# A fourth raw buffer, a third pair and a clock with measured durations in a recorded transformer kernel

## The chip, the cores and the metric

The kernel runs on one core of a Trainium2 chip. One launch computes the whole network. Times are device microseconds (us). The kernel before took 2119.27 us, the median of 3 runs (2117.88 to 2119.61); the profile was taken on one more execution of it, which took 2115.18 us.

The engines are called by their names and by the short names of the profile: TensorE (PE for its matmuls, PEld for its weight loads), VectorE (DVE), ScalarE (ACT), GpSimd (POOL) and SyncE (SP), which issues the DMA transfers.

## The reference

256 latent tokens and 256 context tokens, 1024 channels, float32, two layers. Each layer has a mixer and a PEER stage (a table of 16384 one-row experts per layer), and both are modulated by a vector that comes from the conditioning:

```python
for i in range(DEPTH):                                 # DEPTH = 2
    mod = (c_act @ ada_w[i] + ada_b[i])                # six vectors of 1024: shift, scale, gate, twice
    h = rmsnorm(x, norm1_w[i]) * (1.0 + sc1) + sh1
    if i % 2 == 0:
        y, y_c = mixer_ab(h, h_c, ...)                 # gated DeltaNet (both directions) and attention
    else:
        y = fourier_mix(h) @ w_out_f[j]
    x = x + g1 * y
    x = x + g2 * peer(rmsnorm(x, norm2_w[i]) * (1.0 + sc2) + sh2, peer_wq[i], ...)
return rmsnorm(x, final_norm_w)

def peer(h, w_q, sub_keys, u_tab, v_tab):              # for each block of 128 tokens
    q = (hb @ w_q).reshape(128, 8, 2, 128)
    s = einsum('thpd,hpnd->thpn', q, sub_keys)         # 8 heads, 2 halves, 128 keys each
    s1, i1 = top_k(s[:, :, 0], 16)
    s2, i2 = top_k(s[:, :, 1], 16)
    top_s, pos = top_k(all 256 sums s1 + s2, 16)       # 16 experts for each head
    gate = softmax(top_s)
    act = gelu(einsum('td,thkd->thk', hb, u_tab[idx]))
    return einsum('thk,thkd->td', gate * act, v_tab[idx])
```

## The kernel before

**Stages.** The mixer of layer 0 fills the first 465 us or so. It multiplies with `w_in` (29 weight tiles), builds the modulation vectors from `ada_w` (tiles that pass through the buffers `mraw`), inverts the triangular matrices of the DeltaNet chunks on VectorE, computes the attention, merges, scans, and multiplies with `w_out`. Then come the PEER stage of layer 0 (up to about 1255 us), the Fourier mixer of layer 1, and the PEER stage of layer 1 up to the end. The two PEER stages are the same code and the same order of instructions.

**A weight tile.** All large matrices come in tiles of 128 x 1024 float32, in one `Stream` (line 200) in the order of their use. SyncE's DMA brings a tile into a raw buffer (`loads`, line 214). ScalarE copies it, rounded, to the first half of a pair; VectorE subtracts that from the raw tile and so gets the second half (`cuts`, line 225). This subtraction is called a cut here. `mm3` (line 275) then issues 24 matmuls for the tile: high weights by high and by low activations, and low weights by high activations. A raw buffer comes free after its cut, a pair's halves after their last matmuls. There are three raw buffers and two pairs; a PEER stage lends the stream one more pair, called `wide` in the rows, until it has its own use for it.

**A PEER stage** (line 1396) takes 16 tiles of `w_q` and 128 of the table u, then 128 of the table v. While TensorE runs through the tiles of u, VectorE makes the selection, one generator for each block of 128 tokens (`select`, line 1522). For each head it does two top-16 searches over 128 scores and one over 112 candidates, each with `max`, `max_index` and `match_replace`. It then turns positions into key numbers and normalises the gates. At its end three transposes on TensorE bring the two key numbers and the gates into the buffer `pT`; they are called T0 for token block 0 and T1 for block 1. After that `weigh` (line 1616) makes one-hot factors of `pT` on VectorE, four operations of 128 x 1024 float16 for 8 tokens, TensorE multiplies them, and `spread` (line 1644) multiplies the result into DD, which holds the activations of the experts by expert columns. Columns of u that are stored later are multiplied by their weight when they are stored (`activations`, line 1509). So the fewer columns are stored when `weigh` runs, the smaller are the products of `spread` and the more multiplications `activations` makes.

**What sets the order.** Each engine works through its instructions in the order in which the program recorded them. The program is written as generators ("chains"); `Lanes.run` (line 65) always resumes the chain whose clock stands lowest. The clocks come from `took` (line 98), which gives every recorded instruction an estimated duration. An estimate that is too long or too short therefore changes no arithmetic, only the order on the queues. Two factors stretch VectorE's estimates, `PACE` (line 31): 1.35 in `select`, 1.1 in `weigh`. Every instruction is issued from one line of a helper (133 in this kernel, 127 in the changed one), so lines don't tell instructions apart in the profile; buffers and shapes do.

Of the kernel before, what the change touches and what calls it, by code (L numbers as in the profile page):

```python
# [11 lines left out]
F16 = mybir.dt.float16  # L12
# [13 lines left out]
AHEAD = 6  # L26
SUMMED = 6
LN_EXP = "natural_log_exp_and_others"


PACE = 1.35, 1.1


EARLY = dict(cc=(KC, 2), ada_b=(2, 48), norm1=(2, KC), norm2=(2, KC), norm_f=(KC,))
LATER = dict(conv=(12, 3), unit=(3,), unitw=(2,), headw=(2,), lam=(4,), ones64=(128,), tri=(128,), rot=(128,),
# [14 lines left out]
class Lanes:  # L50
# [5 lines left out]
    def __init__(self, nc):  # L56
        self.nc, self.free, self.cur, self.waiting = nc, {}, None, []
        self.tensor, self.vector, self.scalar, self.gpsimd, self.sync = (
            Lane(self, n) for n in ("tensor", "vector", "scalar", "gpsimd", "sync"))
# [38 lines left out]
    def took(self, eng, op, args):  # L98
        now = self.cur.after(eng) if self.cur else 0.0
        n = max([math.prod(a.shape[1:]) for a in args[:2] if hasattr(a, "shape")], default=0)  # L100
        if eng == "sync":
            self.free[eng] = max(self.free.get(eng, 0.0), now) + n * args[0].shape[0] * 4 / 360e3
            return
        if eng == "tensor":
            n = math.prod(args[0].shape[1:])
            if op == "transpose":
                d = 0.11
            elif args[2].dtype == F32:
                d = n / 2400 if args[0].shape[0] == 32 else n / 600 if n >= 128 else 0.42
            else:  # L110
                d = n / 2400
        elif eng == "vector":
            d = n / (1920 if all(a.dtype == F16 for a in args[:3] if hasattr(a, "dtype")) else 960)
            d = max(d + (0.115 if op.startswith("ma") else 0.07), 0.12)
        else:
            d = n / (1200 if eng == "scalar" else 600) + 0.1
        if self.cur and eng == "vector":
            d *= self.cur.pace
        self.free[eng] = max(self.free.get(eng, 0.0), now) + d
        if self.cur:  # L120
            self.cur.t, self.cur.eng = self.free[eng], eng
# [16 lines left out]
class Chain:  # L138
    def __init__(self, gen, t, low, ground):
        self.gen, self.t, self.low, self.ground, self.on, self.eng = gen, t, low, ground, [], None  # L140
        self.pace = 1.0

    def wait(self, t, eng):
        if t > self.t:
# [55 lines left out]
class Stream:  # L200


    def __init__(self, c, pool, sources):
        self.c, self.n, self.sources = c, 0, sources
        lanes = c.nc
        self.raws = lanes.stock([c.t(pool, [128, 1024], tag=f"raw{i}") for i in range(3)])
        self.parts = [lanes.stock(x) for x in zip(*(c.pair_tiles(pool, f"pair{i}") for i in range(2)))]
        self.raw, self.tile = {}, {}
        self.loaded, self.cut = lanes.events(2, len(sources))
        self.begin = lanes.events(2)  # L210
        lanes.add(self.loads(), ground=True)
        lanes.add(self.cuts(), ground=True)
# [1183 lines left out]
def peer(c, layer, xT, shift, g2, coming, A):  # L1396

    nc = lanes = c.nc
    banks, stream = c.banks, c.stream
    with c.tc.tile_pool(name=f"peer{layer}", bufs=1) as dp:  # L1400
# [7 lines left out]
        x = c.scaled  # L1408
# [3 lines left out]
        def region(j, n):  # L1412
            return DD[:, j:j + n, :].rearrange("p a b -> p (a b)")
# [107 lines left out]

        def select(tb):

            lanes.cur.pace, lanes.cur.low = PACE[0], "vector"
            w = Scratch(region(80 + 12 * tb, 12))
            rep, cand, rep2 = w(128), w(112), w(112)
            tv = w(256).rearrange("p (h s a) -> p h s a", h=8, s=2)
# [62 lines left out]
            n = 2048  # L1590
            while n >= 512:
# [5 lines left out]
                                    op=OP.add)  # L1597
# [18 lines left out]
        def weigh(i):  # L1616


            yield pk
            lanes.cur.pace = PACE[1]  # L1620
            oa, bh, ob = late["onehots"][i]
            for g in range(i, NT // 8, 2):
                i1, i2, hi, lo = (pT[:, n, g * 8:g * 8 + 8].rearrange("p (g t) -> p g t", g=4).unsqueeze(2)
                                  .broadcast_to([128, 4, 128, 2]) for n in range(4))
                iota = c.iota.unsqueeze(1).broadcast_to([128, 4, 128, 2])
                nc.vector.tensor_tensor(oa, i1, iota, op=OP.is_equal)
                yield
                nc.vector.tensor_tensor(ob, i2, iota, op=OP.is_equal)
                yield
                nc.vector.tensor_tensor(bh, ob, hi, op=OP.mult)  # L1630
                yield
                nc.vector.tensor_tensor(ob, ob, lo, op=OP.mult)
                yield
                for f in range(2):
                    ps = yield from banks.take()
                    pt = ps.rearrange("p (t j) -> p t j", t=4)
                    for t in range(4):
                        a, b, d = (x[:, 2 * f + t // 2, :, t % 2] for x in (oa, bh, ob))
                        nc.tensor.matmul(pt[:, t], a, b, start=True, stop=False)
                        nc.tensor.matmul(pt[:, t], a, d, start=False, stop=True)  # L1640
                    lanes.add(spread(2 * g + f, pt, ps))
                    yield

        def spread(e, pt, ps):
            yield ek[e - 1] if e else None
            there = sorted(stored)
            n = 2 * len(there)
            assert there == list(range(len(there)))
            ts = slice(e * 4, e * 4 + 4)
            pt = pt.rearrange("p t j -> p j t")  # L1650
            if n < 128:
                nc.scalar.activation(DD[:, n:, ts], pt[:, n:], AF.Copy, scale=1.0 / GSC)
            nc.vector.scalar_tensor_tensor(DD[:, :n, ts], pt[:, :n], 1.0 / GSC, DD[:, :n, ts], op0=OP.mult, op1=OP.mult)
            banks.give(ps)
            weighed[0] += 4
            ek[e].set()
# [75 lines left out]
        for gen in (normalised(), load_keys(), queries(), weights(), select(0), select(1), weigh(0), weigh(1),  # L1732
                    *(scores(hd) for hd in range(8))):
            lanes.add(gen)
# [154 lines left out]
```

## Time and profile before

| | kernel before |
|---|---|
| median of 3 runs | 2119.27 us (2117.88 to 2119.61) |
| profiled execution, its own time | 2115.18 us |
| span of that execution | 2113.4 us |
| TensorE busy | 2063.5 us, 98% |
| VectorE busy | 1549.2 us, 73% |
| ScalarE busy | 1022.1 us, 48% |
| read from memory | 366.71 MB, 174 GB/s over the span |

The profile describes one execution. The span runs from its first to its last instruction, and the execution's own time is a little longer. Engines work side by side, so busy times don't add up. TensorE is busy in all but 2% of the span, and most of what VectorE and ScalarE do lies beside its matmuls. A window of the trace gives the busy time of each engine in a stretch, the number of instructions that started there, and the clock that TensorE was granted, as a share of its full speed. A timeline gives the instructions of an engine in order, each with its start and duration, and in brackets how long the engine had been idle before it and which engine ended that.

### The profile page before, as it was taken

How to read it: one execution, taken by the hardware profiler on the slowest of the kernel's cores; microseconds unless marked ns; L12 is line 12 of the kernel's file. 1: busy time of each engine (PE TensorE's matmuls, PEld its weight loads, DVE VectorE, ACT ScalarE, POOL GpSimd, SP SyncE). 2: the span in 40 equal slices, each digit the busy share in tenths (PEclk: the TensorE clock that was granted, in tenths of full speed). 3: DMA queues.
4: the chain of work that ended last, by engine and by line, in shares of the span. 5: the costliest groups of instructions: out<-in, count | busy, mean ns of one | idle time of the engine just before them, and what ended most of it. 6: DMA issues, size and time to landing. Idle time of an engine off the chain costs nothing.

```text
span 2113.4 us, 43065 instructions
## 1 busy us (share of the span) xinstructions
PE 2063.5 (98%) x17732; PEld 1933.9 (92%) x17732; DVE 1549.2 (73%) x3039; ACT 1022.1 (48%) x1542; POOL 82.8 (4%) x122
## 2 busy tenths in 40 slices
PE   7999989999999999999999999999999999999998
PEld 3566658989999999999999989999999999999997
DVE  3479978879998999565555556999899956555554
ACT  4443344155545444554444545554544455444453
POOL 3000023000000000000000000000000000000000
PEclk8999999999999999999999999999999999999999
DMA  7655671045565444665655543556544466666553
GB/s 300 213 180 169 232 240 38 1 133 180 189 198 170 142 149 151 198 212 196 192 195 194 193 160 116 172 190 199 170 141 149 150 199 211 195 194 193 196 192 118
DMA packets 102549, 370.65 MB, mean 175 GB/s; under 512 B 11696, under 2 KB 12976, under 8 KB 101968
## 3 DMA queue, kind: packets, MB, share of 16 engines
q1 hardware_dynamic: 102352, 367.90, 53.0%
q8 instruction: 138, 2.26, 0.4%
q14 instruction: 59, 0.48, 0.1%
HBM read 366.71 MB, written 1.15 MB: 174 GB/s over the span
## 4 chain that ended last, share of the span: by engine, by line
PE 79%; DVE 10%; DMA 6%; ACT 3%; issue 1%; POOL 0%; SPq 0%; POOLq 0%; ACTq 0%; DVEq 0%
PE bank L133 79%; DMA raw<-in_u_dram 3%; DVE wide_lo L133 3%; DVE pair L133 2%; DVE wide L133 2%; DMA mraw<-in_ada_w_dram 2%; DVE DD L133 1%; DVE area L133 1%; ACT pair L133 1%; DMA area<-in_ctx_dram 1%; ACT wide L133 0%; ACT DD L133 0%; DMA area<-in_ada_w_dram 0%; ACT bank L133 0%; DVE a L133 0%
## 5 line engine op out<-in xcount | busy, mean ns | idle before, releaser
L133 ACT ACTIVATE pair<-raw 128x1024 fp32r<-128x1024 f32 x376 | 399.1, 1062 | 435.2 <-PE bank L133 342.9
L133 DVE TENSOR_TENSOR pair<-raw,pair 128x1024 fp32r<-128x1024 f32 x376 | 458.1, 1219 | 182.8 <-ACT pair L133 167.1
L133 PE MATMUL bank<-h,pair 128*128 128x256 f32 x4464 | 557.4, 280 | 0.0
L133 PEld LDWEIGHTS bank<-h,pair 128*128 128x128 f32 x4464 | 528.8, 188 | 0.2 <-DVE pair L133 0.2
L133 PE MATMUL bank<-wide,pair 128*128 128x256 f32 (+1 forms) x3456 | 417.1, 277 | 0.0
L133 PEld LDWEIGHTS bank<-wide,pair 128*128 128x128 f32 x3456 | 405.4, 188 | 0.6
L133 PE MATMUL bank<-wide,h 128*128 128x256 f32 x2880 | 336.6, 276 | 0.0
L133 PEld LDWEIGHTS bank<-wide,h 128*128 128x128 f32 x2880 | 331.3, 188 | 0.0
L133 PE MATMUL bank<-h,wide 128*128 128x256 f32 x2160 | 264.5, 277 | 0.0
L133 PEld LDWEIGHTS bank<-h,wide 128*128 128x128 f32 x2160 | 253.7, 188 | 0.0
L133 DVE TENSOR_TENSOR h<-raw,h 128x1024 fp32r<-128x1024 f32 x120 | 147.0, 1225 | 140.1 <-ACT h L133 140.1
L133 ACT ACTIVATE h<-raw 128x1024 fp32r<-128x1024 f32 x120 | 127.4, 1062 | 161.8 <-PE bank L133 149.2
L133 PE MATMUL bank<-S,pair 128*128 128x256 f32 (+1 forms) x888 | 195.5, 362 | 4.2 <-POOL S L133 2.5
L133 PEld LDWEIGHTS bank<-S,pair 128*128 128x128 f32 x888 | 138.8, 199 | 52.3 <-issue 29.9
L133 ACT ACTIVATE DD<-bank 128x512 f32<-128x512 f32 (+25 forms) x284 | 107.6, 394 | 95.8 <-PE bank L133 92.8
L133 ACT ACTIVATE wide<-raw 128x1024 fp32r<-128x1024 f32 x90 | 95.6, 1062 | 106.7 <-PE bank L133 53.3
L133 DVE TENSOR_TENSOR wide<-raw,wide 128x1024 fp32r<-128x1024 f32 x90 | 109.3, 1214 | 2.3 <-ACT wide L133 2.0
L133 DVE TENSOR_TENSOR wide<-DD,wide 128x512 fp32r<-128x512 f32 x128 | 87.3, 684 | 8.3 <-ACT wide L133 8.2
L133 DVE TENSOR_TENSOR DD<-bank,DD 128x512 f32<-128x512 f32 (+13 forms) x84 | 42.3, 504 | 64.8 <-ACT bank L133 61.2
L133 DVE TENSOR_TENSOR wide_lo<-wide_lo,pT 128x1024 f16<-128x1024 f16 x128 | 85.9, 681 | 0.0
L133 ACT ACTIVATE wide<-DD 128x512 fp32r<-128x512 f32 x128 | 78.6, 615 | 9.5 <-PE bank L133 9.5
L133 POOL TENSOR_TENSOR wide_lo<-wide_lo 128x256 f32<-128x256 f32 x10 | 8.3, 834 | 1591.5 <-ACT wide_lo L133 1590.9
(242 smaller groups left out, 1893.7 us busy)
## 6 DMA issues: line engine op xcount, KB each, us to landing
raw<-in_u_dram SPq DMA_DIRECT2D x256, 512.0 KB, 3.5
raw<-in_v_dram SPq DMA_DIRECT2D x256, 512.0 KB, 4.3
mraw<-in_ada_w_dram SPq DMA_DIRECT2D x84, 512.0 KB, 4.2
raw<-in_wq_dram SPq DMA_DIRECT2D x32, 512.0 KB, 3.5
raw<-in_w_in_dram SPq DMA_DIRECT2D x29, 512.0 KB, 4.3
area<-in_ada_w_dram SPq DMA_DIRECT2D x12, 512.0 KB, 6.3
raw<-in_w_out_ab_dram SPq DMA_DIRECT2D x8, 512.0 KB, 4.5
raw<-in_w_out_f_dram SPq DMA_DIRECT2D x8, 512.0 KB, 3.5
```

Source lines behind the costliest of these rows:

```text
L133: return f(*args, **kw)
```

## The change

Three things change.

The stream gets a fourth raw buffer and a third pair. In a PEER stage four pairs serve the stream while it has `wide`, instead of three.

The memory comes from `dynamic_dma_scratch_size=1024`, an argument of the program's constructor that shrinks the area kept for dynamic DMAs. The kernel has none of these.

In `took` the float32r matmuls count n/2257 us instead of n/2400 for n output columns, `max` gets an overhead of 0.175 us, `max_index` 0.14 and `match_replace` 0.25 in place of 0.115, 0.115 and 0.115, and the two factors of `PACE` go.

```diff
-PACE = 1.35, 1.1
...
             elif args[2].dtype == F32:
                 d = n / 2400 if args[0].shape[0] == 32 else n / 600 if n >= 128 else 0.42
             else:
-                d = n / 2400
+                d = n / 2400 if args[2].dtype == F16 else n / 2257
         elif eng == "vector":
             d = n / (1920 if all(a.dtype == F16 for a in args[:3] if hasattr(a, "dtype")) else 960)
-            d = max(d + (0.115 if op.startswith("ma") else 0.07), 0.12)
+            d = max(d + dict(max=0.175, max_index=0.14, match_replace=0.25).get(op, 0.07), 0.12)
         else:
             d = n / (1200 if eng == "scalar" else 600) + 0.1
-        if self.cur and eng == "vector":
-            d *= self.cur.pace
...
-        self.raws = lanes.stock([c.t(pool, [128, 1024], tag=f"raw{i}") for i in range(3)])
-        self.parts = [lanes.stock(x) for x in zip(*(c.pair_tiles(pool, f"pair{i}") for i in range(2)))]
+        self.raws = lanes.stock([c.t(pool, [128, 1024], tag=f"raw{i}") for i in range(4)])
+        self.parts = [lanes.stock(x) for x in zip(*(c.pair_tiles(pool, f"pair{i}") for i in range(3)))]
...
-            lanes.cur.pace, lanes.cur.low = PACE[0], "vector"
+            lanes.cur.low = "vector"
...
-            lanes.cur.pace = PACE[1]
...
-    nc = bacc.Bacc("TRN2", target_bir_lowering=False, num_devices=1)
+    nc = bacc.Bacc("TRN2", target_bir_lowering=False, num_devices=1, dynamic_dma_scratch_size=1024)
```

The clock and the buffers move instructions on every engine. Three places show how. In the rows, names carry a running number; `h` are the activations, `ident` marks a transpose, and x16 counts equal instructions in a row.

The first is TensorE's queue in the PEER stage of layer 0 around T0, the transposes of `DD` by `ident`. Before:

```order
L133 MATMUL bank_3_66<-h_3819,pair_12_75 128x256 x16
L133 MATMUL bank_3_66<-h_3819,pair_13_76 128x256 x8
L133 MATMUL bank_3_66<-h_3819,wide_4041 128x256 x24
L133 MATMUL bank_5_68<-h_3819,pair_14_77 128x256 x4
L133 MATMUL bank_6_69<-ident_82,DD_3818 128x128 x3
L133 MATMUL bank_5_68<-h_3819,pair_14_77 128x256 x12
```

And in the changed kernel:

```order
L127 MATMUL bank_6_69<-h_3825,pair_13_76 128x256 x16
L127 MATMUL bank_6_69<-h_3825,pair_14_77 128x256 x8
L127 MATMUL bank_6_69<-h_3825,wide_4051 128x256 x24
L127 MATMUL bank_4_67<-ident_85,DD_3824 128x128 x2
L127 MATMUL bank_5_68<-h_3825,pair_15_78 128x256
L127 MATMUL bank_4_67<-ident_85,DD_3824 128x128
L127 MATMUL bank_5_68<-h_3825,pair_15_78 128x256 x15
```

The rows look alike, but from the first score matmul to T0 the queue holds 748 weight-tile matmuls before and 608 now; from T0 to T1 it holds 776 and 649.

The second is VectorE's queue in the selection of that layer, where the cuts (`TENSOR_TENSOR` with a raw buffer) stand between the operations of the top-16 searches. Before:

```order
L133 TENSOR_TENSOR pair_15_78<-raw_10_73,pair_14_77 128x1024
L133 MAX_INDEX DD_3818<-DD_3818 128x8
L133 MAX DD_3818<-DD_3818 128x8
L133 MAX_INDEX DD_3818<-DD_3818 128x8
L133 MATCH_REPLACE DD_3818<-DD_3818 128x128
L133 MAX DD_3818<-DD_3818 128x8
L133 TENSOR_TENSOR pair_13_76<-raw_11_74,pair_12_75 128x1024
```

And in the changed kernel:

```order
L127 TENSOR_TENSOR wide_4051<-raw_11_74,wide_4051 128x1024
L127 MAX_INDEX DD_3824<-DD_3824 128x8
L127 MAX DD_3824<-DD_3824 128x8
L127 MAX_INDEX DD_3824<-DD_3824 128x8
L127 MATCH_REPLACE DD_3824<-DD_3824 128x128
L127 MAX DD_3824<-DD_3824 128x8
L127 MAX_INDEX DD_3824<-DD_3824 128x8
L127 MAX DD_3824<-DD_3824 128x8
L127 MAX_INDEX DD_3824<-DD_3824 128x8
L127 TENSOR_TENSOR pair_16_79<-raw_12_75,pair_15_78 128x1024
```

More operations of the search now stand between two cuts: up to T0 there are 30 cuts before and 26 now, from T0 to T1 32 and 26.

The third is TensorE's queue near the end of the mixer, where the inverse (`area`, 64x64) is transposed. Before, modulation tiles (`mraw`) stand between the transposes:

```order
L133 MATMUL bank_3_66<-ident_82,area_29_108 64x64 x8
L133 MATMUL bank_2_65<-ident_82,area_29_108 64x64 x8
L133 MATMUL bank_7_70<-ident_82,area_29_108 64x64 x8
L133 MATMUL bank_6_69<-mraw_37_116,cact_88 32x256 x4
L133 MATMUL bank_5_68<-ident_82,area_29_108 64x64 x8
L133 MATMUL bank_4_67<-ident_82,area_29_108 64x64 x8
L133 MATMUL bank_6_69<-mraw_36_115,cact_88 32x256 x4
```

In the changed kernel the last modulation tile stands ahead of them, among the products of the attention:

```order
L127 MATMUL bank_6_69<-mraw_40_119,cact_91 32x256 x4
L127 MATMUL bank_7_70<-ident_85,wide_lo_116 128x128 x4
L127 MATMUL bank_4_67<-area_31_110,bq_123 128x512
L127 MATMUL bank_2_65<-ident_85,mrow_117 128x128 x4
L127 MATMUL bank_1_64<-wide_lo_116,area_31_110 128x128 x4
L127 MATMUL bank_6_69<-area_31_110,bq_123 128x512
L127 MATMUL bank_5_68<-ident_85,area_32_111 64x64 x8
L127 MATMUL bank_4_67<-ident_85,area_32_111 64x64 x3
L127 MATMUL bank_7_70<-ident_85,wide_lo_116 128x128 x4
L127 MATMUL bank_4_67<-ident_85,area_32_111 64x64 x5
```

Of the 84 modulation tiles that use the two `mraw` buffers, 45 are used before the last projection matmul of 512 columns in the kernel before and 56 now; behind the last projection matmul stand 10 before and 2 now.

## Rows read from the trace of the kernel before

**Rows 1.** The page's first part: busy us, share of the span, instructions.

```profile
PE 2063.5 (98%) x17732; PEld 1933.9 (92%) x17732; DVE 1549.2 (73%) x3039; ACT 1022.1 (48%) x1542; POOL 82.8 (4%) x122
```

**Rows 2.** A window: its us, busy us (and starts) by engine, clock, DMA share, GB/s.

```profile
850.00:900.00 50.00, 50.00 (x443) 50.00 (x442) 27.80 (x30) 25.38 (x29) 0.00 (x0) 1.00 0.61 193
```

**Rows 3.** Windows of the mixer in which TensorE is idle at times.

```profile
200.00:250.00 50.00, 45.88 (x337) 31.92 (x329) 47.84 (x70) 17.96 (x34) 0.79 (x1) 0.93 0.66 219
250.00:300.00 50.00, 46.05 (x329) 29.27 (x322) 37.17 (x76) 23.36 (x52) 11.76 (x14) 0.93 0.73 249
300.00:350.00 50.00, 45.86 (x446) 35.59 (x445) 43.57 (x94) 25.68 (x58) 18.89 (x32) 1.00 0.37 120
```

**Rows 4.** Windows: selection of block 0, of block 1, one-hot products.

```profile
481.36:568.36 87.00, 87.00 (x760) 86.91 (x759) 82.31 (x280) 47.68 (x64) 0.00 (x0) 1.00 0.57 187
568.36:655.95 87.59, 87.59 (x774) 87.59 (x773) 82.31 (x272) 44.56 (x52) 0.00 (x0) 1.00 0.59 193
...
662.51:837.89 175.38, 173.15 (x1694) 169.12 (x1693) 164.17 (x260) 86.21 (x159) 0.00 (x0) 1.00 0.45 145
```

**Rows 5.** TensorE's timeline: start us, us, instruction (scores, T0, T1, first product).

```profile
478.28 1.95 PE L133 MATMUL bank<-DD 128*128 128x128 f32 x16
...
571.50 0.49 PE L133 MATMUL bank<-ident,DD 128*128 128x128 f32 x3
...
659.99 0.49 PE L133 MATMUL bank<-ident,DD 128*128 128x128 f32 x3
...
670.31 0.63 PE L133 MATMUL bank<-wide_lo 128*128 128x128 f16 x8
```

**Rows 6.** VectorE's timeline: normalisations, copy to pT, a cut, one-hot factors.

```profile
568.07 0.29 DVE L133 TENSOR_TENSOR DD<-DD 128x128 f32<-128x128 f32 x1
...
655.66 0.29 DVE L133 TENSOR_TENSOR DD<-DD 128x128 f32<-128x128 f32 x1
...
660.52 0.43 DVE L133 CAST pT<-bank 128x256 f16<-128x256 f32 x1 [3.00 <-PE bank L133]
...
661.38 1.21 DVE L133 TENSOR_TENSOR pair<-raw,pair 128x1024 fp32r<-128x1024 f32 x1
662.51 0.68 DVE L133 TENSOR_TENSOR wide_lo<-pT,iota 128x1024 f16<-128x1024 f16 x1
...
663.72 0.68 DVE L133 TENSOR_TENSOR wide_lo<-pT,iota 128x1024 f16<-128x1024 f16 x1
```

**Rows 7.** Layer 1, timelines of VectorE and TensorE: normalisation and T0.

```profile
1414.01 0.29 DVE L133 TENSOR_TENSOR DD<-DD 128x128 f32<-128x128 f32 x1
...
1417.36 0.49 PE L133 MATMUL bank<-ident,DD 128*128 128x128 f32 x3
```

**Rows 8.** Groups by form, 450 to 860: busy us, mean ns, idle before.

```profile
L133 DVE SCALAR_TENSOR_TENSOR DD<-bank,DD 128x400 f32<-128x400 f32 x3 | 1.7, 562 | 0.0
L133 DVE SCALAR_TENSOR_TENSOR DD<-bank,DD 128x248 f32<-128x248 f32 x4 | 1.6, 406 | 0.0
L133 DVE TENSOR_TENSOR DD<-bank,DD 128x512 f32<-128x512 f32 x4 | 2.8, 691 | 5.4 <-ACT bank L133 5.4
...
L133 PE MATMUL bank<-wide_lo 128*128 128x128 f16 x256 | 21.6, 220 | 1.9 <-DVE wide_lo L133 1.7
L133 PE MATMUL bank<-wide_lo,a 128*128 128x128 f16 x256 | 21.2, 220 | 0.3 <-DVE wide_lo L133 0.2
```

**Rows 9.** TensorE's waits, 200 to 335: us in total, times, longest.

```profile
PE bank L133 <- DMA mraw<-in_ada_w_dram: 4.3, 5, 2.5
PE bank L133 <- DVE bq L133: 4.0, 1, 4.0
```

**Rows 10.** The page's DMA queues: packets, MB, share of 16 engines.

```profile
q1 hardware_dynamic: 102352, 367.90, 53.0%
```

**Rows 11.** Windows around that wait for a rotated query.

```profile
213.00:218.00 5.00, 0.96 (x7) 0.76 (x7) 5.00 (x8) 1.11 (x2) 0.00 (x0) 0.98 0.87 315
218.00:225.00 7.00, 7.00 (x30) 3.46 (x30) 5.56 (x8) 0.78 (x2) 0.00 (x0) 0.53 0.55 192
```

More of the change, by code (lines that the diff above doesn't have):

```diff
@@ L140, in __init__ @@
         self.gen, self.t, self.low, self.ground, self.on, self.eng = gen, t, low, ground, [], None
-        self.pace = 1.0
     def wait(self, t, eng):
```

## The prediction

> **What bounds the kernel now.** I read the page's engine totals first: TensorE is busy for 2063.5 of 2113.4 us [rows 1], so no change can win more than about 50 us without taking matmuls away, and none goes. Then the table of 50 us windows. In 850 to 900 us TensorE starts 443 matmuls in 50.00 busy us, 0.1129 us each [rows 2]; the windows around it, and nearly all of 500 to 650, 850 to 1250 and 1700 to 2100, read the same. There another buffer has nothing to give. What can move is the mixer, the first 450 us, where TensorE idles visibly [rows 3], and the stretch of each PEER layer in which VectorE does the top-k and the one-hot products beside the weight cuts. In layer 0 that is 481 to 838 us, and VectorE is busy for 82.31 of 87.00, 82.31 of 87.59 and 164.17 of 175.38 us there [rows 4], while TensorE has no idle time in the first two. VectorE is the second bound, hidden only as long as its results arrive before TensorE's queue comes to them. So I read the timeline at the three places where TensorE needs a result of the selection: the transposes T0 and T1 that end the selection of token block 0 and 1, and the first one-hot product.
>
> In before each comes late enough. The normalisation that T0 transposes ends at 568.07 + 0.29 = 568.36, T0 starts at 571.50: 3.1 us spare. The one for T1 ends at 655.95, T1 starts at 659.99: 4.0 spare. The third factor of the first one-hot product ends at 663.72 + 0.68 = 664.40, the product starts at 670.31: 5.9 spare [rows 5, 6]. Layer 1 repeats it: 1414.30 against 1417.36 [rows 7].
>
> **The change, part by part.** *The order of the selection.* The new clock gives VectorE's selection no factor of 1.35 and its one-hot work none of 1.1, so the recorder believes that it ends sooner and puts T0, T1 and the products earlier on TensorE's in-order queue. I counted both orders. From the first score matmul to T0 TensorE has 748 weight-tile matmuls before and 608 after; from T0 to T1 776 and 649; from T1 to the first product 88 and 64; from the first to the last product 1133 and 1103. VectorE's top-k instructions in these stretches are as many as before; only cuts leave them: 30 become 26 up to T0, 32 become 26 up to T1, 2 stay 2, and 48 become 46 in the products. A cut costs VectorE 662.51 - 661.38 = 1.13 us, start to start [rows 6].
>
> The Trainium skill, "VectorE: DVE Perf Modes", section "The DRAIN you can't avoid", says that the next instruction does not start until the pipeline is empty; the row shows the next one starting 0.08 us before the recorded end of a 1.21 us cut. By the rule the ten cuts that leave before T1 would save 12.1 us instead of 11.3, and the sum would be 1.6 us lower over two layers; the row decides.
>
> T0: TensorE arrives 140 x 0.1129 = 15.8 us earlier, at 555.7. VectorE loses four cuts, 4.5 us, and is done at 563.8. Wait 8.1 us where there was none. It is shorter by whatever idle time VectorE gives up in that stretch, 87.00 - 82.31 = 4.7 at most: 3.4 to 8.1.
> T1, counted from T0: TensorE needs 88.49 - 127 x 0.1129 = 74.2 us, VectorE 87.59 - 6 x 1.13 = 80.8. Wait 6.6, or 1.3 if all 5.28 us of idle time go.
> Together 4.7 to 14.7 us a layer. Much of the idle time is slivers between dependent instructions, which stay, and some is waits for TensorE, which go when TensorE is the one ahead; I take half, 9.8. Queued behind the waiting transposes are all the weight-tile matmuls, so nothing hides the wait, and matmuls put off are not given back later: TensorE is full after it.
> First product: TensorE needs 10.32 - 24 x 0.1129 = 7.6 us from T1. VectorE's copy starts 0.53 us after T1, and from there to 664.40 took 3.88: 4.4 us. No wait.
>
> *The products.* TensorE's 175.38 us of 662.51 to 837.89 hold 2.23 idle [rows 4]; 30 matmuls fewer leave 172.0. Without any wait it is 1103 x 0.1129 plus 21.6 + 21.2 us of one-hot products [rows 8] = 167.3. VectorE loses two cuts (2.3 us), and its scalings of the one-hot results shrink from 19000 to 15624 elements a partition, since fewer expert columns are stored by then: (562 - 406) / 152 = 1.03 ns an element [rows 8], 3.5 us. It needs 169.6 with its idle time of before and 158.4 without: beside TensorE's work either way. This gives back 0 to 4.7 us; I take 2, TensorE's visible idle time.
> A layer then costs 9.8 - 2 = 7.8 us, two layers 15.6.
>
> *Seven more multiplications a layer* stand on VectorE after the products, 0.69 us each at most [rows 8]. There VectorE is busy for 27.80 of 50 us [rows 2]: nothing. Without that cover it would be 4.8 us a layer.
>
> *The fourth raw buffer and the third pair* also let transfers and cuts of the mixer run further ahead, and the order shows what follows: of the 84 modulation tiles that pass through the two mraw buffers, 56 instead of 45 are used before the last 512-wide projection matmul, and 2 instead of 10 stand behind the last projection matmul, where the transposes of the inverse wait for nothing else. TensorE idles for 4.1, 3.9 and 4.1 us in 200 to 350 [rows 3]; mraw transfers end 4.3 us of it and a rotated query 4.0 [rows 9]. VectorE's work for that query stands as before, so its wait stays. The transfers' waits may go (-4.3), come back earlier in the queue in the same size (0), or double because raw loads now share the DMA queue with them (+4.3); all idle time gone would be -12.2. I take -4, the row's wait.
>
> *The scratch memory* costs nothing: the data move on the queue q1 [rows 10], whose DMAs SyncE issues, and the shift of addresses by whole 4 KB tiles changes no instruction.
>
> **Sum.** The profiled execution took 2115.18 us, 1.8 of it outside its span of 2113.4; the median of the runs is 2119.27, 4.1 more. 2115.2 + 15.6 - 4 = 2126.8 for such an execution, 2131 for the median.
>
> **Rivals.** *Hidden anyway*: VectorE gives up all its idle time before T0 and T1, so the waits are 4.7 a layer, and the products give back 2.2. With the mixer's -4 that is 2119.3 + 5 - 4 = 2120. For it: part of the idle time is 1 to 3 us gaps that end on other engines. Against: a layer's two stretches would need VectorE busy for 100%, which no window shows.
>
> *The mixer wins*: the moved modulation tiles let TensorE close all 12.2 us of 200 to 350, while each layer's waits and gains cancel (4.7 - 4.7). 2119.3 - 12.2 = 2107, faster. It decides as soon as a layer costs under about 4 us, half of what I take. For it: ten tiles leave a stretch in which TensorE waits for transfers. Against: a third of those waits are VectorE's.
>
> *The clock falls*: TensorE idled for 4.0 us of 213 to 218, and in 218 to 225 the granted clock was 0.53, nearly all at the lower level, 1.2 GHz [rows 11]. My waits for T0 and T1 are as long. Each such stretch would cost 7 x 0.47 = 3.3 us; four of them 13, 2144 in all. Against: after T0 TensorE is ahead of VectorE again, so a slow stretch shortens the wait for T1 instead of adding to it. The Trainium skill, "TensorE: Matmul & The Clock Gate", section "What's actually happening", has a gate that passes half of the pulses once the engine has been idle and opens again when it is busy; the rows agree, and by that rule alone all four would be paid.
>
> **How the numbers follow.** The forecast, 2131 with its own range of 2121 to 2141, has 0.50; hidden 0.17, the mixer 0.21, the clock 0.12. The bounds of the terms reach from 2107 to 2153 (14.7 a layer with nothing given back, and +4.3 in the mixer). Half of the mixer's chance and less of the clock's may be left out: 2108 to 2147. About 0.2% (4.2 us) is what a measurement of this kernel can tell from no change. Faster by more is the mixer's 0.21; within it are most of hidden and the low end of the forecast, 0.19; slower 0.60.
>
> **What would show it.** In the changed profile TensorE should come to T0 some 77 us after the first scores (571.50 - 478.28 [rows 5], less 15.8) and wait there 3 to 8 us for a VectorE result, again at T1 1 to 7 us, in both layers, with VectorE busier than 95% before them; the window of the products should be shorter by about 5 us, and modulation tiles should be used up before the mixer's inverse is transposed. If TensorE shows no wait at T0, the clock's durations or my count of VectorE's work are wrong and the kernel is not slower; if the granted clock falls behind each wait, the time is near 2144.

## The result and the profile after

The changed kernel took 2131.48 us, the median of 6 runs (2130.38 to 2133.58); beside them the kernel before took 2118.15 (6 runs). The ratio of the comparison is 1.0071, with an interval of 1.0054 to 1.0088: slower by 11 to 19 us. (Dividing the two medians gives 1.0063, within that interval.) The forecast was 2131.

The page's first part, and TensorE's waits from 450 to 860 us (us in total, times, longest). Before, that stretch held one line of waits, 1.9 us for `wide_lo`.

```profile
PE 2066.5 (97%) x17732; PEld 1936.9 (91%) x17732; DVE 1552.4 (73%) x3053; ACT 1026.0 (48%) x1542; POOL 87.8 (4%) x122
...
PE bank L127 <- DVE DD L127: 9.7, 3, 4.7
```

TensorE is busy 3.0 us longer than in [rows 1], in a span 16.0 us longer (2129.4). The new line is a wait for the selection (`DD`). TensorE's timeline shows it: first scores, T0, T1 and first one-hot product of layer 0, which answer to [rows 5], then T0 and T1 of layer 1.

```profile
473.06 1.17 PE L127 MATMUL bank<-DD 128*128 128x128 f32 x9
...
555.42 0.69 PE L127 MATMUL bank<-ident,DD 128*128 128x128 f32 x2 [4.73 <-DVE DD L127]
555.76 0.56 PE L127 MATMUL bank<-h,pair 128*128 128x256 f32 x1
557.32 0.47 PE L127 MATMUL bank<-ident,DD 128*128 128x128 f32 x1 [0.99 <-DVE DD L127]
...
637.99 0.51 PE L127 MATMUL bank<-ident,DD 128*128 128x128 f32 x2 [3.99 <-DVE DD L127]
...
647.47 0.29 PE L127 MATMUL bank<-wide_lo 128*128 128x128 f16 x2
...
1409.68 0.69 PE L127 MATMUL bank<-ident,DD 128*128 128x128 f32 x2 [4.72 <-DVE DD L127]
...
1491.82 0.69 PE L127 MATMUL bank<-ident,DD 128*128 128x128 f32 x2 [3.98 <-DVE DD L127]
```

T0 came apart: two transposes wait for the key numbers, the third, one matmul later, for the gates. VectorE's windows from the first search to the end of the normalisation of block 0, from there to that of block 1, and the one-hot products; then the mixer's windows. They answer to [rows 4] and [rows 3].

```profile
476.62:557.26 80.64, 74.98 (x646) 74.29 (x644) 77.95 (x278) 42.21 (x58) 0.00 (x0) 0.97 0.51 171
557.26:638.69 81.43, 77.38 (x653) 77.19 (x654) 76.53 (x267) 37.43 (x43) 0.00 (x0) 0.96 0.52 173
641.73:810.08 168.35, 168.35 (x1664) 165.64 (x1664) 160.77 (x262) 88.73 (x159) 0.00 (x0) 1.00 0.44 149
200.00:250.00 50.00, 46.77 (x341) 31.62 (x340) 50.00 (x63) 14.86 (x23) 0.00 (x0) 1.00 0.70 230
250.00:300.00 50.00, 47.53 (x327) 29.96 (x326) 41.00 (x85) 27.24 (x63) 11.37 (x14) 1.00 0.70 232
300.00:350.00 50.00, 46.26 (x420) 38.00 (x420) 43.68 (x96) 28.16 (x64) 20.47 (x31) 0.97 0.16 55
```

TensorE is idle for 5.7 and 4.1 us in the two windows of the selection, where it had none; its clock is below 1 in both; VectorE is busy for 96.7% and 94.0% of them, where the prediction looked for more than 95%. The window of the products is 7.0 us shorter than in [rows 4], where about 5 was said.

The loss is read stage by stage: what TensorE needed in before, less 0.1129 us for each weight-tile matmul that has left the stage, against what it took. The last product ends at 809.67 + 0.63 = 810.30; in before the row was the second one here.

```profile
809.67 0.63 PE L127 MATMUL bank<-wide_lo,a 128*128 128x128 f16 x8
```

```profile
838.93 0.98 PE L133 MATMUL bank<-wide_lo,a 128*128 128x128 f16 x14
```

| layer 0 | before, less the matmuls that left | after | lost |
|---|---|---|---|
| scores to T0 | 93.22 - 15.81 = 77.41 | 82.36 | 4.95 |
| T0 to T1 | 88.49 - 14.34 = 74.15 | 82.57 | 8.42 |
| T1 to first product | 10.32 - 2.71 = 7.61 | 9.48 | 1.87 |
| products to the last one's end | 169.60 - 3.39 = 166.21 | 162.83 | -3.38 |
| sum | | | 11.9 |

Layer 1 gives 4.8, 8.2, 1.7 and -3.4, together 11.4. Both layers: 23.2 us, against 15.6 forecast. The rest of the 16.0 lies outside: the first scores stand 5.2 us earlier (478.28 to 473.06, 0.9 of it because 8 matmuls fewer stand ahead of them), and from the last product of layer 0 to the scores of layer 1, the Fourier stage among it, 3.3 us are gained (484.1 us before, 36.2 more for the 321 matmuls that come after the products now, and 517.0 measured). That leaves 0.4 for the end.

### The profile page after: what moved, and what is told of

Read it like the earlier page. It is cut to its first block, busy times and chain, and to the rows that moved or that the text cites. A ratio compares the mean times of both kernels' runs of the same rounds, so it can differ in the third digit from the quotient of the medians.

```text
span 2129.4 us, 43210 instructions
## 1 busy us (share of the span) xinstructions
PE 2066.5 (97%) x17732; PEld 1936.9 (91%) x17732; DVE 1552.4 (73%) x3053; ACT 1026.0 (48%) x1542; POOL 87.8 (4%) x122
## 4 chain that ended last, share of the span: by engine, by line
PE 85%; DVE 11%; DMA 2%; issue 1%; ACT 1%; POOL 0%; SPq 0%; POOLq 0%; DVEq 0%; ACTq 0%
PE bank L127 85%; DVE DD L127 4%; DVE pair L127 3%; DVE wide L127 2%; DVE area L127 1%; DMA mraw<-in_ada_w_dram 1%; DMA area<-in_ada_w_dram 1%; DVE wide_lo L127 0%; DVE bq L127 0%; POOL area L127 0%; DVE sm L127 0%; DMA x<-in_x_dram 0%; ACT pair L127 0%; DVE h L127 0%; DMA raw<-in_w_out_f_dram 0%
## 5 line engine op out<-in xcount | busy, mean ns | idle before, releaser
L127 DVE TENSOR_TENSOR pair<-raw,pair 128x1024 fp32r<-128x1024 f32 x423 | 514.1, 1219 | 213.4 <-ACT pair L127 191.7
L127 PE MATMUL bank<-h,pair 128*128 128x256 f32 x4992 | 616.9, 281 | 0.0
L127 PEld LDWEIGHTS bank<-h,pair 128*128 128x128 f32 x4992 | 591.8, 189 | 0.0
L127 PE MATMUL bank<-wide,pair 128*128 128x256 f32 (+1 forms) x4032 | 479.7, 277 | 0.0
L127 PEld LDWEIGHTS bank<-wide,pair 128*128 128x128 f32 x4032 | 469.4, 188 | 0.1
L127 PE MATMUL bank<-wide,h 128*128 128x256 f32 x2304 | 269.4, 276 | 0.0
L127 PEld LDWEIGHTS bank<-wide,h 128*128 128x128 f32 x2304 | 265.1, 188 | 0.0
L127 PE MATMUL bank<-h,wide 128*128 128x256 f32 x1632 | 209.0, 281 | 0.0
L127 PEld LDWEIGHTS bank<-h,wide 128*128 128x128 f32 x1632 | 196.9, 190 | 0.0
L127 ACT ACTIVATE DD<-bank 128x256 f32<-128x256 f32 (+17 forms) x270 | 107.1, 405 | 70.0 <-PE bank L127 62.8
L127 DVE TENSOR_TENSOR wide<-DD,wide 128x512 fp32r<-128x512 f32 x128 | 87.5, 684 | 11.2 <-ACT wide L127 8.2
```

What stands on the lines that cost most here:

```text
L127: return f(*args, **kw)
```

## The experiments

The kernel before ran beside each of them; its medians were 2115.1 to 2115.9 us. The theory (A): the order that the new clock makes brings TensorE to T0 and T1 before VectorE has finished the selection, and the buffers give a little back. Rivals: the buffers cost the time; the waits are hidden or only move; the clock's falls cost it.

**Clock alone** (e1): the changed kernel with

```diff
-        self.raws = lanes.stock([c.t(pool, [128, 1024], tag=f"raw{i}") for i in range(4)])
+        self.raws = lanes.stock([c.t(pool, [128, 1024], tag=f"raw{i}") for i in range(3)])
-        self.parts = [lanes.stock(x) for x in zip(*(c.pair_tiles(pool, f"pair{i}") for i in range(3)))]
+        self.parts = [lanes.stock(x) for x in zip(*(c.pair_tiles(pool, f"pair{i}") for i in range(2)))]
```

> The changed clock with the three raw buffers and two pairs of before (the scratch argument stays). Its order has 594 weight-tile matmuls from the first scores to T0 (608 in the changed kernel), 630 from T0 to T1 (649), 24 and 27 cuts there (26 and 26). Theory A, the order of the selection makes TensorE wait: waits of some 5 us at T0 and 7 at T1, 24 us in two layers, the clock falling behind them as in the changed kernel (10 us for both layers), 7 given back in the products, and none of the buffers' gain: 2118 + 24 + 10 - 7 = 2145, between 2135 and 2150, so slower than the changed kernel. Theory B, the buffers cost the time and the clock nothing: within 5 us of 2118. A time near 2131 would say that the buffers do nothing either way.

Measured 2166.17 us, ratio 1.0242 (1.0227 to 1.0257). The sign is that of the theory, the size is far beyond it: 51 us over before, some 20 more than expected. Its trace has the waits for `DD` at T0 and T1 in both layers (16.0 us), and the first scores stand at 488.62, 10.3 later than in before. Read stage by stage as in the table above, its layers lost 14.0 and 17.7 us, against 11.9 and 11.4 in the changed kernel; so the loss is larger in the mixer and in both layers.

**Buffers alone** (e2): the kernel before with the buffers and the scratch argument of the change.

```diff
-... tag=f"raw{i}") for i in range(3)])
+... tag=f"raw{i}") for i in range(4)])
-... f"pair{i}") for i in range(2)))]
+... f"pair{i}") for i in range(3)))]
```

> Four raw buffers, three pairs and the scratch argument, with the clock of before (PACE 1.35 and 1.1). T0 has 756 matmuls ahead of it and T1 796, with 31 and 33 cuts. Theory A: no wait of TensorE at T0 and T1 in either layer, PEER stages as long as in before, and the mixer and the Fourier stage shorter by 3 to 9 us together: 2109 to 2115. Theory B, the buffers cost the time: about 2131. Theory C, buffers hidden anyway: 2118 within 3 us.

Measured 2123.95 us, ratio 1.0038 (1.0024 to 1.0052). TensorE has no wait for `DD` and the PEER layers are as long as in before; but the buffers gave nothing by themselves, they cost 8 us. The first scores stand at 483.94, 5.7 later. That part of the theory fell: what a buffer is worth depends on the order that the clock makes with it.

**T0 and T1 placed 8 us later** (e3): the changed kernel with one line ahead of the transposes.

```diff
+            yield lanes.cur.t + 8.0, None
             ps = yield from banks.take()
             nc.tensor.transpose(ps[:, 0:128], it[:, :128], c.ident)
```

> The changed kernel, but the recorder holds the chain back by 8 us of its clock just ahead of the three transposes at the end of each selection, so that T0 stands behind 676 weight-tile matmuls instead of 608 (7.7 us more) and T1 behind 7.1 us more; VectorE's order up to them is nearly the same. Theory A, TensorE waits because it comes too early and loses the clock behind the wait: both waits (9.7 us a layer) go and the clock stays up (5 us of falls a layer), nothing else changes: 2131 - 2 x 9.7 - 10 = 2102, between 2100 and 2113. Rival, VectorE bounds the selection and the products as a whole, so a wait removed at T0 and T1 comes back at the one-hot products: 2126 to 2133, with waits for wide_lo of 8 us or more a layer.

Measured 2127.45 us, ratio 1.0053 (1.0038 to 1.0067). TensorE's timeline at T0, T1 and the first products:

```profile
563.67 0.49 PE L127 MATMUL bank<-ident,DD 128*128 128x128 f32 x3
...
643.26 0.49 PE L127 MATMUL bank<-ident,DD 128*128 128x128 f32 x3
...
653.73 0.22 PE L127 MATMUL bank<-wide_lo 128*128 128x128 f16 x1 [1.60 <-DVE wide_lo L127]
654.94 0.56 PE L127 MATMUL bank<-wide_lo 128*128 128x128 f16 x7 [0.99 <-DVE wide_lo L127]
```

No bracket is left at T0 and T1, but the first products wait for VectorE instead, and from T0 to T1 TensorE still took 79.59 us where 644 matmuls and its pace in before make 73.6. The profile names 1.6 us of short waits there, 1.3 for cuts and 0.3 for a copy of ScalarE, and doesn't name the rest; the clock is 1.00 there. The layers lost 6.1 and 8.0 us instead of 11.9 and 11.4. The rival was right for more than half: most of the loss moved with the transposes, though the waits for `wide_lo` are 2.6 and 3.2 us a layer and not 8.

**TensorE kept busy in the waits** (e4): the changed kernel with

```diff
             ps = yield from banks.take()
+            for j in range((54, 40)[tb]):
+                nc.tensor.eng.matmul(ps[:, :NT], h[0][:, j % KC, :128], h[0][:, j % KC, :NT], start=True, stop=True)
```

> The changed kernel with 54 matmuls that nobody reads in front of T0 and 40 in front of T1, in the bank that the transposes then overwrite; the recorder does not count them. They take 54 x 0.113 = 6.1 and 4.5 us, about as long as TensorE waits there (the three transposes now stand together and need the last result, 6.5 and 4.7 us after TensorE's arrival). So the time until the transposes is the same, but TensorE is busy in it. Theory A with the clock: the granted clock no longer falls to half behind T0 and T1, which gives back 3 to 5 us a layer, 2121 to 2126 in all. Rival, the falls have another cause than the idle time, or cost nothing because TensorE waits for VectorE there anyway: 2129 to 2133.

Measured 2130.64 us, ratio 1.0078 (1.0062 to 1.0094), no less than the changed kernel. Windows of 7 us from T0 on, the changed kernel first, this one second:

```profile
555.42:562.42 7.00, 6.00 (x27) 5.71 (x28) 6.24 (x23) 1.06 (x1) 0.00 (x0) 0.50 0.56 200
```

```profile
554.00:561.00 7.00, 7.00 (x61) 6.90 (x61) 6.72 (x27) 2.43 (x3) 0.00 (x0) 1.00 0.44 153
```

Behind the idle time the granted clock is 0.50, the lower level, 1.2 GHz; behind the filled one it is 1.00, and 61 matmuls start instead of 27. So the idle time made it fall. But scores to scores took 854.63 us here and 854.26 in the changed kernel. What TensorE gained behind T0 it waited out ahead of T1, for the same VectorE results. The rival's time came, by its second reason. Behind T1 the filling kept the clock up in layer 1 alone. Windows of e4 from T1 to the first product, layer 0 and layer 1, with 68 weight-tile matmuls each:

```profile
633.97:644.23 10.26, 9.94 (x72) 9.67 (x72) 9.92 (x17) 2.61 (x3) 0.00 (x0) 0.83 0.58 189
1488.89:1497.58 8.69, 8.37 (x72) 8.10 (x72) 8.59 (x16) 2.61 (x3) 0.00 (x0) 1.00 0.56 177
```

There the fall was mostly paid: 1.6 us up to the first product, of which 1.1 are left at the end of the last one (173.8 against 172.7 us from T1).

After these four the theory was narrower (A2): VectorE's selection and products set the end of their stretch, and only more TensorE work ahead of T0 and T1, or less VectorE work, helps.

**The two factors put back** (e5, 1.35 and 1.1; e6, 1.2 and 1.0), on the changed kernel:

```diff
+PACE = 1.35, 1.1
...
+        if self.cur and eng == "vector":
+            d *= self.cur.pace
...
-            lanes.cur.low = "vector"
+            lanes.cur.pace, lanes.cur.low = PACE[0], "vector"
...
+            lanes.cur.pace = PACE[1]
```

> The changed kernel with the two PACE factors, 1.35 in the selection and 1.1 in the products, put back on top of the new durations; buffers and mixer order are those of the changed kernel. T0 has 852 weight-tile matmuls ahead of it, T1 864 more, with 36 and 35 cuts. Theory A2, formed after e1 to e4: in the changed kernel VectorE's selection and products set the end of their stretch, so a wait removed at one place partly comes back at the next (e3), and the falls of the clock behind a wait cost nothing of their own (e4); only more weight-tile matmuls ahead of T0 and T1 help. Then the PEER layers are as short as in before (scores of layer 0 to the end about 21 us shorter than in the changed kernel, no wait at T0 and T1): ratio to before 0.995 to 1.002. Rival, the extra buffers make the PEER layers or the mixer slower whatever the clock does (e2 was 0.4% slower than before): ratio 1.003 to 1.007.

Measured 2107.85 us, ratio 0.9966 (0.9954 to 0.9978).

> As e5, with factors 1.2 in the selection and 1.0 in the products: 720 matmuls to T0, 748 to T1, 30 and 31 cuts, so TensorE comes to T0 3.2 us earlier than in before with VectorE's work as in before, and there were 3.1 us to spare; at T1 4.0 were to spare and about 2 are used up. Theory A2: no wait or under 1 us at T0 and T1, PEER layers within 2 us of before, the whole within 3 us of e5. Rival, the estimate of the spare time is too coarse and waits of 3 us or more remain: 6 us or more above e5.

Measured 2106.54 us, ratio 0.9955 (0.9940 to 0.9970). This version beats both kernels. Windows from the scores of layer 0 to those of layer 1 and from there to the end, of e6 and of the changed kernel:

```profile
476.75:1317.70 840.95, 839.69 (x7475) 831.92 (x7474) 621.82 (x1157) 432.21 (x609) 9.24 (x10) 1.00 0.54 178
1317.70:2106.60 788.90, 778.52 (x7006) 774.59 (x7004) 577.05 (x1071) 391.39 (x525) 3.66 (x5) 1.00 0.54 177
```

```profile
473.06:1327.32 854.26, 843.45 (x7475) 835.42 (x7474) 622.90 (x1162) 433.47 (x608) 9.25 (x10) 0.99 0.53 175
1327.32:2129.40 802.08, 782.33 (x7006) 777.61 (x7004) 577.59 (x1076) 392.76 (x524) 3.65 (x5) 0.99 0.53 175
```

The same matmuls, and 13.3 and 13.2 us less time. In e6 the profile names no wait of TensorE between 465 and 870. The rival (the extra buffers cost) is out: both have them.

**New durations alone** (e7): e5 with the buffers of before.

```diff
-... tag=f"raw{i}") for i in range(4)])
+... tag=f"raw{i}") for i in range(3)])
-... f"pair{i}") for i in range(3)))]
+... f"pair{i}") for i in range(2)))]
```

> The new durations alone: three raw buffers and two pairs, PACE 1.35 and 1.1 as in before. 832 matmuls to T0, 868 to T1. It differs from e1 (51 us slower than before) by PACE alone. Theory A2: the waits of the PEER layers (16 us of waits for DD in e1) go, and with them about 36 us of PEER time; what remains of e1's loss is the mixer's, about 10: ratio 1.000 to 1.008. Rival, the new durations are what costs, in the mixer and in the layers: ratio above 1.012.

Measured 2132.32 us, ratio 1.0079 (1.0062 to 1.0097): the upper end of what was expected. Against e1, which lacks PACE only, it is 34 us (36 expected). It is still 17 us over before; the first scores stand at 486.88, 8.6 later.

**Scratch alone** (e8): the kernel before with

```diff
-    nc = bacc.Bacc("TRN2", target_bir_lowering=False, num_devices=1)
+    nc = bacc.Bacc("TRN2", target_bir_lowering=False, num_devices=1, dynamic_dma_scratch_size=1024)
```

> The kernel before with the smaller scratch area alone; its order is that of before, instruction for instruction. All theories: same time within 0.2%. Its trace is a second look at the order of before, and shows by how much the mixer varies from one execution to the next (the first scores stood at 478.28 in before; at 473.06, 478.43 and 470.30 in the three traces with the mixer order of the changed kernel): within 5 us, 473 to 483.

Measured 2116.03 us, ratio 1.0004 (0.9994 to 1.0014); first scores at 478.31. The two traces of the order of before agree within 0.03 us there. The mixer order of the changed kernel stands in seven traces (after, e3 to e6, and e9 and e10 below), and in them the first scores stood at 473.06, 478.43, 470.30, 477.38, 476.75, 477.97 and 475.00: 475.6 in the mean, 8.1 between the ends.

**Less work for VectorE at the same places** (e9): the changed kernel with

```diff
-                nc.vector.scalar_tensor_tensor(
-                    e[:, a].rearrange("p (n k) -> p n k", k=16), abf.rearrange("p h s k -> p (h s) k"), float(a),
-                    tft[:, :, a:a + 1].broadcast_to([128, 16, 16]), op0=OP.is_equal, op1=OP.mult)
+                args = (e[:, a].rearrange("p (n k) -> p n k", k=16), abf.rearrange("p h s k -> p (h s) k"), float(a),
+                        tft[:, :, a:a + 1].broadcast_to([128, 16, 16]))
+                if a < 8:
+                    nc.vector.scalar_tensor_tensor(*args, op0=OP.is_equal, op1=OP.mult)
+                else:
+                    lanes.took("vector", "scalar_tensor_tensor", args)
...
-                nc.vector.tensor_tensor(eq[:, :n], eq[:, :n], eq[:, n:2 * n], op=OP.add)
+                args = eq[:, :n], eq[:, :n], eq[:, n:2 * n]
+                if n < 2048:
+                    nc.vector.tensor_tensor(*args, op=OP.add)
+                else:
+                    lanes.took("vector", "tensor_tensor", args)
```

> The changed kernel without the upper half of the gather that turns positions into key numbers: 8 of 16 one-hot operations and the first addition are left out of each selection (part of the experts' numbers are therefore not those of the reference), while the recorder still counts them, so that T0 and T1 stand where they stand in the changed kernel. VectorE's selection of a block is shorter by 8 x 0.35 + 1.15 = 3.9 us. Theory A2, TensorE's loss at T0 and T1 (6.6 and 8.4 us behind its own pace, in layer 0) is VectorE's time and nothing else: 7.8 us a layer come back, 15.7 in all, ratio to before 1.0071 - 0.0074 = 0.9997, between 0.998 and 1.002. Rival, the loss is made by the placing itself (clock, queue) or comes back in the products: less than half of it, ratio 1.004 or more.

Measured 2119.61 us, ratio 1.0024 (1.0012 to 1.0036): 10 of the 15.7 us came back by the ratios. That is just above the range expected, and below the rival's 1.004. TensorE's waits from 465 to 870:

```profile
PE bank L127 <- DVE DD L127: 3.3, 4, 1.5
PE bank L127 <- DVE wide_lo L127: 0.3, 1, 0.3
```

T0 comes 78.45 us after the scores instead of 82.36, and T1 77.75 after T0 instead of 82.57 (9 matmuls fewer, 1.0 us). With the stages read as in the table, the layers' losses fall from 11.9 and 11.4 to 3.5 and 3.7 us: 16 us back, as expected. In this trace the first scores stand 4.9 us later than in the changed kernel's, within the spread above, and the Fourier stage is 3 us longer, as it was in e3; whether that accounts for the smaller gain of the whole time was not tried apart.

**Factors between** (e10): e5 with

```diff
-PACE = 1.35, 1.1
+PACE = 1.1, 1.0
```

> As e6, with factors 1.1 and 1.0: T0 behind 664 weight-tile matmuls, T1 behind 696 more, 28 and 29 cuts (608, 649, 26 and 26 in the changed kernel; 720, 748, 30 and 31 in e6). Two ways to work out the waits. VectorE keeps its idle time: it took 80.6 us from the first search to the normalisation in the changed kernel and takes 2 x 1.13 more here; TensorE comes 56 x 0.113 = 6.3 us later; 6.6 - 6.3 + 2.3 = 2.6 us are lost at T0, 8.4 - 5.3 + 3.4 = 6.5 at T1, 9 a layer where e6 loses 1: 16 us over e6, ratio 1.003. VectorE gives up half of its idle time, as the prediction had it: 4 us a layer, 6 over e6, ratio 0.998.

Measured 2117.89 us, ratio 1.0020 (1.0008 to 1.0033). That is 13.8 us over e6 by the ratios and 11.0 by the medians, each over its own kernel before, and the two intervals are 5 and 6 us wide: the time does not decide between the sum in which VectorE keeps its idle time (16) and the one that lets it give up half (6). Waits for `DD`, 465 to 870:

```profile
PE bank L130 <- DVE DD L130: 4.3, 4, 1.5
```

The trace, read as in the table, has 5.2 us lost at T0 and T1 together in layer 0 and 5.5 in layer 1, where the first sum has 9 a layer and the second 4. VectorE's windows of the selection of blocks 0 and 1:

```profile
478.56:561.93 83.37, 80.91 (x701) 80.44 (x699) 80.58 (x280) 45.07 (x61) 0.00 (x0) 1.00 0.54 178
561.93:645.28 83.35, 81.55 (x703) 81.16 (x703) 80.14 (x270) 40.31 (x46) 0.00 (x0) 0.98 0.57 184
```

It kept 2.8 and 3.2 us of idle time here. So neither sum holds: part of that time is given up, and how much changes with the order.

**One buffer at a time** beside the durations and PACE: e5 with two pairs (e11), and e5 with three raw buffers (e12).

```diff
-... f"pair{i}") for i in range(3)))]
+... f"pair{i}") for i in range(2)))]
```

```diff
-... tag=f"raw{i}") for i in range(4)])
+... tag=f"raw{i}") for i in range(3)])
```

> e5 with two pairs instead of three: the fourth raw buffer alone beside the new durations and PACE (e7 has neither buffer, ratio 1.0079; e5 both, 0.9966). Its order is nearly that of e7 (832 matmuls to T0, 868 to T1, 34 and 37 cuts), so by the theory that buffers act through the order that they allow, it is near e7: ratio 1.004 to 1.009. Rival, a transfer that starts earlier is what counts: near e5, below 1.000.

Measured 2116.86 us, ratio 1.0016 (1.0004 to 1.0028): 13 us below e7 with nearly e7's order, which the theory of the order did not foresee, and 11 above e5, which the rival did not. ScalarE's waits in the products of layer 0, e7 (692 to 870; e11, 682 to 855, has no line for `raw`):

```profile
ACT wide L130 <- DMA raw<-in_u_dram: 17.0, 9, 3.2
ACT pair L130 <- DMA raw<-in_u_dram: 14.9, 14, 2.5
```

A copy that waits for a transfer makes the cut late, and VectorE is idle for 11.2 of those 178 us in e7 and for 6.6 of 173 in e11; that the transfers start earlier with a fourth raw buffer is the likely reason. The products, read as in the table, took 165.28 us in e11 and 170.14 in e7, for one weight-tile matmul fewer. But this is not the whole of it: of the 16.1 us between the two spans 9.0 lie ahead of the first scores (477.88 against 486.88). And e5, the faster version, has 25.3 us of such waits in its products, so they alone don't put the versions in order.

> e5 with three raw buffers instead of four: the third pair alone beside the new durations and PACE. Its order is nearly that of e5 (852 and 864 matmuls, 36 and 35 cuts). By the theory that buffers act through the order, it is near e5: ratio 0.995 to 0.999. Rival, the fourth raw buffer is what counts: 1.003 or more.

Measured 2112.07 us, ratio 0.9987 (0.9975 to 1.0000): near e5, 4 us above it and at the upper end of what was expected.

All together, as ratios to the kernel before:

| | 3 raw, 2 pairs | 4 raw, 3 pairs |
|---|---|---|
| old durations, PACE 1.35 and 1.1 | 1 | 1.0038 |
| new durations, PACE 1.35 and 1.1 | 1.0079 | 0.9966 |
| new durations, no PACE | 1.0242 | 1.0071 |

The old durations without PACE were not run.

## Why the prediction was right, and where not

**The sum** was 2131, and 2131.48 came, but three terms were off and cancelled. The layers' term was 15.6 and measured 23.2; outside the layers -4 was forecast, and the trace shows -7.2 (-4.3 in the mixer, -3.3 around the Fourier stage, 0.4 at the end). So the profiled execution took 2131.13, 4.3 more than the 2126.8 forecast for it. The 4.1 added from there to the median made that good, and in the changed kernel the median stands only 0.35 above the profiled execution. That the time came out within 1 us is luck.

**The step that mattered was right**: without PACE the transposes come too early for VectorE. The right column of the last table gives its price, 1.0071 against 0.9966, 22 us; e9, e10 and e6 show that it is VectorE's time that TensorE waits for. TensorE came to T0 555.42 - 4.73 - 473.06 = 77.6 us after the scores (77 forecast) and waited 4.73 us, then 0.99 for the third transpose, 5.7 of the 3.4 to 8.1 forecast.

**The term that was mis-sized** is the idle time of VectorE: "I take half, 9.8". VectorE had 4.69 and 5.28 us of it [rows 4] and kept 80.64 - 77.95 = 2.69 and 81.43 - 76.53 = 4.90, 2.6 more than half. Its busy time was mis-sized too: ahead of T1 it fell from 82.31 to 76.53, by 5.8 us, where six cuts were to take 6.8 away. So VectorE took 81.43 us there; the forecast with no idle time given up was 80.8. T0 and T1 together cost 4.95 + 8.42 = 13.4 us in layer 0, near the upper end of the range of 4.7 to 14.7, where the middle was taken. In another order half comes close: e1, which lacks the buffers, kept 79.32 - 76.38 = 2.94 and 79.87 - 77.29 = 2.58. The waits that the profile names are only 9.7, because behind T0 the slow clock stretched TensorE's own work into the wait for T1.

**From T1 to the first product** no wait was forecast, and 1.9 us were lost; behind T1 the clock was at its lower level again for 3.4 us in both layers, and e4 shows that such a fall is paid for there (10.26 us against 8.69).

**The products** gave back 3.4 us a layer, forecast 2 out of 0 to 4.7. The seven more multiplications a layer did no harm: behind the products TensorE is busy throughout, as before.

**The mixer**: -4 was put on the transfers of modulation tiles, and their waits in 200 to 335 did fall from 4.3 [rows 9] to 0.7, and the query's from 4.0 to 2.0. But e8, whose order is that of before, has 8.0 and 1.9 us there, with the first scores where before has them: such a row of one execution is no price, and the query's fall is not the change's. TensorE's idle time in 200 to 350 fell from 12.2 to 9.4, and none of that is seen at the end of the mixer: where the stretch of `w_out` begins both kernels stand at 426.4, and some 4.5 us come behind it, where the clock did not fall in the changed kernel's trace. In 426.4 to 450 it is 1.00 there and in e4 and e10, and 0.93 in e3, e5, e6 and e9, which have the same mixer order. Rows: that stretch, after and before.

```profile
426.40:458.70 32.30, 28.59 (x238) 27.28 (x237) 28.13 (x48) 17.80 (x39) 4.75 (x5) 1.00 0.38 127
```

```profile
426.40:463.40 37.00, 32.33 (x242) 30.68 (x241) 29.01 (x48) 18.79 (x39) 3.68 (x5) 0.91 0.35 119
```

Over the seven traces the gain is 478.3 - 475.6 - 0.9 = 1.8 us. The size was right in one trace by luck. That it belongs to the buffers is not shown: e2 has the buffers and a slower mixer.

**The rivals.** *Hidden anyway* and *the mixer wins* did not come. *The clock falls* did, behind T0 and T1 in both layers, and yet the time was not 2144. The reason given against it held behind T0: a slow stretch shortens the next wait. Behind T1, with no such wait ahead, the fall was mostly paid. The falls themselves agree with the rule that the prediction cited from the Trainium skill ("TensorE: Matmul & The Clock Gate", "What's actually happening"): half of the clock behind the idle time, 0.50 in the rows of e4's comparison, and the full one where there was none. That each fall is paid does not follow from it, and for the falls behind T0 e4 shows the contrary.

**The scratch memory** cost nothing (1.0004).

Left open: which part of VectorE's idle time closes; what the clock still leaves out, so that with measured durations and no PACE the transposes come too early; and why the new durations make the mixer slower with three raw buffers and two pairs (e7), and the old ones with four and three (e2). Which lines of the clock do it was not tried.

## What to carry to other kernels

When one engine's queue is ordered by a clock, a factor that looks like a fudge may hold the distance at which another engine's results arrive; measured durations alone did not replace it here. Idle time of an engine that is the second bound is only in part a reserve: of 10.0 us before the two transposes, 5.5 (e1), 6.0 (e10) and 7.6 (the changed kernel) stayed once TensorE waited for VectorE. A wait removed by moving one instruction comes back at the next, when the engine behind it is late as a whole, so take work away from that engine or put other work ahead of the wait.

## What the hardware showed unexpectedly

A fall of TensorE's clock can be free where a wait for another engine follows. With the idle time filled the clock stayed at 1.00 instead of 0.50 behind T0, and scores to scores took 854.63 us instead of 854.26.

The one mixer order gave first scores from 470.30 to 478.43 us in seven executions; between 426.4 and 450 us the clock stayed at 1.00 in three of them and not in the other four.
